# A transformer layer's output projection on Trainium2: loads issued earlier, scales made a tile ahead, stores on another queue, and the first up-projection slices without GpSimd

## The chip, the cores and the metric

The kernel runs on one core of a Trainium2 chip. A core has five engines with a fixed instruction order each: PE (TensorE, matrix products; its weight loads are shown apart as PEld), DVE (VectorE), ACT (ScalarE), POOL (GpSimd) and SP (SyncE, which here only issues transfers). They run beside each other and wait for one another through semaphores. Transfers between device memory and the core's own memory are issued by SP, ACT or POOL and carried by 16 DMA engines. The metric is the device time of one execution in microseconds (us); the time before is 3184.6, the median of 3 runs (3182.1 to 3186.07).

## The reference

One encoder layer over 2048 tokens of width 1024 (and 16 meta tokens ahead of them): two mixers side by side, latent attention with 8 heads and a bidirectional S5 state-space model, 512 channels each, then an output projection, and an MLP with squared ReLU. Cut to what the change touches:

```python
mix = jnp.concatenate([rms_norm(attn, g_mix[:512]), rms_norm(ssm, g_mix[512:])], axis=-1)
h = h + rms_norm(mix @ w_out, g_post_mix)
m = rms_norm(h, g_pre_mlp) @ w_mlp_up
m = jnp.square(jax.nn.relu(m)) @ w_mlp_down
h = h + rms_norm(m, g_post_mlp)
```

where `rms_norm(x, g)` is `x * rsqrt(mean(x²) + eps) * g`.

## The kernel before

**Stages.** Input projection; attention head by head with the S5 model woven in as a background task; the output projection with its norms; the MLP, whose up-projection starts with slices cut from the normed hidden state; the down-projection. All products are of float32 quality made from two halves: `split` (lines 124 to 126) rounds a tile to its high part on ACT (names with h: sh, ah, T00h) and subtracts that on DVE or POOL for the low part (sl, al, T00l); each product is then three matrix products (high·high, high·low, low·high).

**Memory scratch.** Attention writes its output, not yet divided, to AD and the sums of its weights to RD; after the last head of a block of 512 tokens the sums are read back, inverted on DVE (rr, line 648) and written to RD2. S5's gated output goes to SD. The residual after the output projection goes to HD, its normed and transposed form to HTD, from which the up-projection reads.

**The output projection** goes over 16 tiles of 128 tokens, t = 0 to 15. For each:

- `s_ops(t)` (line 1115) loads SD's columns into sr and makes sh, sl and sq, the per-token column sums of squares (square on ACT, sum on DVE, lines 1111 and 1112). sr has one buffer.
- `a_ops(t)` (line 1121) loads AD's columns into ar (two buffers) and the inverted sums, spread over partitions, into rb (one buffer, two transfers), multiplies them on DVE (line 1130), and makes ah, al and aq in the same way.
- `out_s(t)` makes S5's part of the projection, 24 products into two banks of 512 columns each (op, line 1184); `out_tile(t)` makes attention's part, 24 more into two other banks.
- The two RMS scales of a tile come from sq and aq: two tiny products with ones (ss, lines 1202 and 1203), a copy to s2c on DVE (line 1205), then on POOL a multiply-add and a power each (rs_v and rs_r, lines 131 and 132).
- For each 512 columns ACT multiplies attention's part by its scale (ot, line 1213) and DVE adds S5's part with its own (o, line 1214, two a tile). A square with its sum on ACT (jk, line 1218), a POOL scale, two DVE operations (lines 1220 and 1221, the gain gpo and the residual xt), the store to HD (line 1222), another square (line 1227), a POOL scale, and hn on DVE (line 1229).
- `hn_T(t)` transposes hn on PE (hT, line 1240) two tiles later, ACT copies it to hb (line 1245), and SP stores it to HTD (line 1246).

**Queues.** Every transfer of this stage is issued by SP, in one order: loads of sr, ar, rb and xt (lines 1118, 1124, 1128 and 1198) and the stores to HD and HTD. A transfer whose buffer or data isn't ready holds up those behind it in this order.

**The bridge to the MLP.** `t_slice(ct, k)` reads a slice traw of HTD (1 MB; line 1275) and makes seven split combinations of its four parts (T0k to T6k). Of its 11 subtractions 4 are on POOL (the splits of b11 and b22, and T1 and T4, lines 1312 and 1315), 7 on DVE. The weights' combinations st (line 1266) are on POOL too. The up-projection's products (p, line 1331) follow.

**What sets the order.** The order in which the code is written gives each instruction a place, and a scheduler with a timeline of its own moves instructions of an engine past each other ahead of the run; on the chip each engine's order is fixed. The results of products live in eight banks that are handed out in turn (`pa`), so a product can also wait for the reader of the bank's previous content.

Of the kernel before, what the change touches and what calls it, by code (L numbers as in the profile page):

```python
# [51 lines left out]
def hymba_layer_kernel(  # L52
# [71 lines left out]
    def split(src, h, l, eng=V):  # L124
        S.copy(out=h, in_=src)  # L125
        eng.tensor_tensor(out=l, in0=src, in1=f(h), op=ALU.subtract)  # L126
# [968 lines left out]
    def out_open():  # L1095
        ip = W["ip"] = ph.enter_context(pool("iO", 2, "right"))
        W["ep"] = ph.enter_context(pool("eO", 2, "right"))
        e1 = W["e1"] = ph.enter_context(pool("e1", 1, "right"))
        gpo = W["gpo"] = mk(e1, [128, D], "gpo")
        Y.dma_start(out=gpo, in_=g_post_mix[0].partition_broadcast(128))  # L1100
        for t in range(2):
            W["s", t] = s_ops(t)
            yield

    def halves(src, nm):

# [4 lines left out]
        S.activation(out=src, in_=src, func=AF.Square)  # L1111
        V.reduce_sum(out=sq, in_=src.rearrange("p k c -> p c k"), axis=AX.X)
        return h, l, sq

    def s_ops(t):
        cs = slice(t * 128, (t + 1) * 128)
        sr = W["ip"].tile([128, 4, 128], F32, tag="sr", name="sr", bufs=1)
        Y.dma_start(out=sr, in_=SD[:, cs].rearrange("(k p) c -> p k c", p=128))
        return halves(sr, "s")

    def a_ops(t):
        cs = slice(t * 128, (t + 1) * 128)
        ar = W["ip"].tile([128, 4, 128], F32, tag="ar", name="ar")
        Y.dma_start(out=ar, in_=AD[:, cs].rearrange("(k p) c -> p k c", p=128))
        rb = W["ip"].tile([128, 4, 128], F32, tag="rb", name="rb", bufs=1)
        for b in range(2):
            src = RD2[b:b + 1, cs]
            Y.dma_start(out=rb[64 * b:64 * b + 64],
                        in_=bass.AP(src.tensor, src.offset, [[0, 64], [2 * 2048, 4], [1, 128]]))
        V.tensor_tensor(out=ar, in0=ar, in1=rb, op=ALU.mult)  # L1130
# [48 lines left out]
    def out_mm(h, l, w0, half):
        hs = slice(half * 512, (half + 1) * 512)  # L1180
        p = pa("op")
        for k in range(4):
            for i, (a, b) in enumerate(((h, W["woh"]), (h, W["wol"]), (l, W["woh"]))):
                T.matmul(out=p, lhsT=a[:, k], rhs=b[:, w0 + k, hs], start=(k == 0 and i == 0),
                         stop=(k == 3 and i == 2))
        return p

    def out_s(t):
        h, l, sq = W.pop(("s", t))
        return sq, [out_mm(h, l, 4, half) for half in range(2)]  # L1190

    def out_tile(t, between):
        if t + 1 < NT:
            W["a", t + 1] = a_ops(t + 1)
        if t + 2 < NT:
            W["s", t + 2] = s_ops(t + 2)
        xt = W["e1"].tile([128, D], F32, tag="xt", name="xt")
        Y.dma_start(out=xt, in_=xv[t // 8, t % 8])
# [2 lines left out]
        p = pa("ss")
        T.matmul(out=p[:, 0:2], lhsT=sqa, rhs=ones)
        T.matmul(out=p[:, 2:4], lhsT=sqs, rhs=ones)
        s2 = sm.tile([128, 4], F32, tag="s2c", name="s2c")
        V.tensor_copy(s2, p[:, 0:4])
        ra = rstd_of(s2[:, 0:1], 512)
        rb = rstd_of(s2[:, 2:3], 512, eps=4 * EPS)
        o = W["ep"].tile([128, D], F32, tag="o", name="o")
        for half in range(2):
# [4 lines left out]
            V.scalar_tensor_tensor(out=o[:, hs], in0=ps[half], scalar=rb, in1=tm, op0=ALU.mult, op1=ALU.add)
# [5 lines left out]
        V.scalar_tensor_tensor(out=o, in0=o, scalar=r, in1=W["gpo"], op0=ALU.mult, op1=ALU.mult)  # L1220
        V.tensor_tensor(out=o, in0=o, in1=xt, op=ALU.add)
# [7 lines left out]
        V.scalar_tensor_tensor(out=hn, in0=o, scalar=r, in1=gpr, op0=ALU.mult, op1=ALU.mult)  # L1229
        return hn  # L1230

    def hn_T(t, hn):

        ct, i = t // 8, t % 8
        cs = slice((i % 4) * 128, (i % 4) * 128 + 128)
        ps = []
        for a in range(2):
# [4 lines left out]
            ps.append(p)
        b = hn if t == NT - 1 else mk(tq, [128, D], "hb")
        for a in range(2):
            S.copy(out=b[:, a * 512:(a + 1) * 512], in_=ps[a])
            Y.dma_start(out=HTD[ct].rearrange("k p b c -> p k b c")[:, :, 2 * a + i // 4, cs],
                        in_=b[:, a * 512:(a + 1) * 512].rearrange("p (k c) -> p k c", k=4))
# [29 lines left out]
    W["a", 0] = a_ops(0)
    for t in range(2):
        W["ps", t] = out_s(t)
    last = []  # L1280
    prep = up_prep(0)
    facs = []
# [20 lines left out]
        for n in range(7):  # L1303
            TB[n, k] = (mk(tb, [128, 512], f"T{n}{k}h", F32R), mk(tb, [128, 512], f"T{n}{k}l", F32R))

    def t_slice(ct, k):
# [4 lines left out]
        split(b11, *TB[B11, k], G)
        G.tensor_tensor(out=l[T1], in0=b12, in1=b11, op=ALU.subtract)
        V.tensor_tensor(out=l[T3], in0=b22, in1=b12, op=ALU.subtract)
        V.tensor_tensor(out=l[T2], in0=b22, in1=l[T1], op=ALU.subtract)
# [256 lines left out]
```

## Time and profile before

| what | value |
|---|---|
| median of 3 runs | 3184.6 us |
| the profiled execution's own time | 3184.3 us |
| its span in the profile | 3182.5 us |
| mean granted PE clock | 0.977 |
| PE, DVE, ACT, POOL busy, share of the span | 95%, 60%, 49%, 40% |
| from the first multiplication ar·rb (line 1130) to the first o of tile 15 (line 1214) | 1558.8 to 1821.3 us |
| PE busy in 1540 to 1900 us | 295.0 of 360 us |

The rows of the trace that are quoted below are of three kinds. A timeline row has the start and the length in us, the engine, the line of the kernel, the operation, the tile written and the tiles read, and in brackets how long the engine was idle before and what ended that. A row of the groups has the number of instructions, their busy time and the mean in ns. A row of a stretch has busy times by engine, the granted PE clock and the share of the DMA engines. SPq marks SP's issue of a transfer.

### The profile page before, as it was taken

What the parts mean: (1) busy time and instruction counts of PE and PEld (TensorE: products, weight loads), DVE (VectorE), ACT (ScalarE), POOL (GpSimd) and SP (SyncE); (2) the same over time, 40 slices, a digit from 0 to 9 for tenths busy, and PEclk for the clock granted to TensorE, in tenths of its full rate; (3) what the DMA queues carried; (4) which work ended last, traced back from release to release, by engine and by line L of the source; (5) the groups of instructions that cost most, each with busy time, mean ns of one, the idle gap of its engine ahead of it and who ended that gap; (6) DMA issues with size and microseconds to landing.
All of it is one profiled execution on the core that took longest, in us unless ns stands there. A gap on an engine that the chain in (4) does not pass through costs nothing. (4 is left out here: it accounts for less than half of the span.)

```text
span 3182.5 us, 42348 instructions
## 1 busy us (share of the span) xinstructions
PE 3017.4 (95%) x14455; PEld 2412.5 (76%) x14455; DVE 1914.8 (60%) x2989; ACT 1563.2 (49%) x2985; POOL 1268.3 (40%) x2363
## 2 busy tenths in 40 slices
PE   6999988899999999999879789998999999999998
PEld 5899965566777766788657568886888888888887
DVE  6333278888888889875356584449444234444447
ACT  4333346777777789864335455455544421111112
POOL 4221255776888887600032275457443000000002
PEclk8999989999999999999989889999999999999999
DMA  4232241111001123231356443333332422222216
GB/s 151 65 86 69 63 91 29 53 45 41 18 19 27 27 70 94 72 122 50 67 137 191 145 149 122 106 107 112 125 106 100 137 79 76 73 76 76 67 63 205
DMA packets 244377, 279.51 MB, mean 88 GB/s; under 512 B 35920, under 2 KB 180688, under 8 KB 243136
## 3 DMA queue, kind: packets, MB, share of 16 engines
q1 hardware_dynamic: 242112, 275.10, 28.5%
q8 instruction: 113, 1.85, 0.2%
q10 hardware_dynamic: 1792, 1.57, 0.2%
q14 instruction: 104, 0.85, 0.1%
q0 software_dynamic: 256, 0.14, 0.0%
HBM read 181.31 MB, written 95.36 MB: 87 GB/s over the span
## 5 line engine op out<-in xcount | busy, mean ns | idle before, releaser
L623 ACT ACTIVATE ph<-s 128x512 fp32r<-128x512 f32 (+1 forms) x544 | 324.1, 596 | 201.6 <-PE s L621 187.5
L627 DVE TENSOR_TENSOR pl<-s,ph 128x512 fp32r<-128x512 f32 x512 | 349.5, 684 | 110.5 <-ACT s L626 108.3
L1516 PE MATMUL dn<-dh,ah 128*128 128x512 f32 x1024 | 398.3, 389 | 0.0
L1516 PE MATMUL dn<-dl,ah 128*128 128x512 f32 x1024 | 398.3, 389 | 0.0
L1516 PE MATMUL dn<-dh,al 128*128 128x512 f32 x1024 | 398.2, 389 | 0.0
L574 DVE TENSOR_REDUCE mx<-mxp 128x1 f32<-128x512 f32 x512 | 342.9, 684 | 47.7 <-PE mxp L573 44.2
L626 ACT ACTIVATE s<-s 128x512 f32<-128x512 f32 x512 | 303.6, 593 | 0.7
L125 ACT CAST ah<-mraw 128x512 fp32r<-128x512 f32 x128 | 79.5, 621 | 449.9 <-DMA mraw<-MD 269.4
L1500 POOL TENSOR_TENSOR ss<-s2f 128x1 f32<-128x1 f32 x16 | 11.2, 699 | 702.2 <-ACT jk L1497 702.2
L1266 POOL TENSOR_TENSOR st<-raw 128x512 f32<-128x512 f32 x128 | 174.0, 1359 | 263.6 <-DVE al L126 263.5
L1521 DVE TENSOR_TENSOR acc<-dn,acc 128x512 f32<-128x512 f32 x224 | 153.3, 688 | 137.6 <-PE dn L1516 137.6
L611 PE MATMUL X<-pl,vt 128*65 128x512 f32 x512 | 207.3, 405 | 25.7 <-DVE pl L627 23.8
L619 PE MATMUL s<-ql,kh 96*128 96x512 f32 (+1 forms) x544 | 224.1, 412 | 4.1 <-ACT o L641 2.6
L1516 PEld LDWEIGHTS dn<-dh,ah 128*128 128x128 f32 x1024 | 192.2, 188 | 39.9
L1516 PEld LDWEIGHTS dn<-dh,al 128*128 128x128 f32 x1024 | 192.2, 188 | 39.9
L1516 PEld LDWEIGHTS dn<-dl,ah 128*128 128x128 f32 x1024 | 192.2, 188 | 39.9
L620 PE MATMUL s<-qh,kl 96*128 96x512 f32 (+1 forms) x544 | 217.2, 399 | 0.0
L621 PE MATMUL s<-qh,kh 97*128 97x512 f32 (+1 forms) x544 | 213.4, 399 | 0.0
L612 PE MATMUL X<-ph,vt 128*64 128x512 f32 x512 | 203.3, 397 | 0.0
L613 PE MATMUL X<-ph,vt 128*65 128x512 f32 x512 | 202.9, 396 | 0.0
L126 DVE TENSOR_TENSOR al<-mraw,ah 128x512 fp32r<-128x512 f32 x128 | 88.4, 691 | 189.8 <-ACT ah L125 179.7
L573 PE MATMUL mxp<-kh,qh 96*128 96x512 f32 x512 | 196.4, 405 | 5.4 <-DVE mx L574 1.9
(813 smaller groups left out, 7819.2 us busy)
## 6 DMA issues: line engine op xcount, KB each, us to landing
raw<-in_w_mlp_up_dram SPq DMA_DIRECT2D x32, 1024.0 KB
MD<-r SPq DMA_DIRECT2D x128, 256.0 KB
mraw<-MD SPq DMA_DIRECT2D x128, 256.0 KB
xt<-in_x_dram SPq DMA_DIRECT2D x32, 512.0 KB
raw<-in_w_mlp_down_dram SPq DMA_DIRECT2D x32, 512.0 KB
ug<-UD SPq DMA_DIRECT2D x32, 256.0 KB
HD<-o SPq DMA_DIRECT2D x16, 512.0 KB
traw<-HTD SPq DMA_DIRECT2D x8, 1024.0 KB
```

Of the source, the lines that this page charges most:

```text
L573: T.matmul(out=p, lhsT=qs[n][0][0:96, j * 128:(j + 1) * 128], rhs=kh[0:96, b * 512:(b + 1) * 512])
L574: V.reduce_max(out=mxs[n][:, j, b:b + 1], in_=p, axis=AX.X)
L611: T.matmul(out=X[:65], lhsT=v[:, t, 0:65], rhs=pl_, start=(t == 0), stop=False)
L612: T.matmul(out=X[:64], lhsT=v[:, t, 65:129], rhs=ph_, start=False, stop=False)
L613: T.matmul(out=X[:65], lhsT=v[:, t, 0:65], rhs=ph_, start=False, stop=False)
L619: T.matmul(out=s[:m], lhsT=kh[0:96, cs], rhs=ql, start=True, stop=False)
L620: T.matmul(out=s[:m], lhsT=kl[:, cs], rhs=qh[0:96], start=False, stop=False)
L621: T.matmul(out=s[:m], lhsT=kh[:, cs], rhs=qh, start=False, stop=True)
L623: S.activation(out=ph_[:m], in_=s[:m], func=AF.Exp, scale=SCALE)
L626: S.activation(out=s, in_=s, func=AF.Exp, scale=SCALE)
L627: V.tensor_tensor(out=pl_, in0=s, in1=f(ph_), op=ALU.subtract)
L1516: T.matmul(out=p, lhsT=a[:, ts_], rhs=c[:, hs], start=(q == 0 and w == 0), stop=(q == FB - 1 and w == 2))
```

## The change

What it does, part by part:

1. A new `loads(t)` issues the loads of sr, xt, ar and rb of a tile up to two tiles ahead of its use; xt, rb and sr now have two buffers instead of one (ar had two). `sd_load` makes the load of sr by itself.
2. A new `scales(t + 1)` makes the next tile's two RMS scales inside tile t, ahead of the transposes; s2c's copy moves from DVE to ACT.
3. `out_s(0)` is written ahead of attention's last products, `out_s(1)` behind them.
4. The store to HD moves from SP's queue to ACT's, behind the second square, and the stores to HTD move from SP's to ACT's.
5. The four slices of ct = 0 make all 11 subtractions on DVE; those of ct = 1 stay as they were.

```diff
+    def sd_load(t):
+        cs = slice(t * 128, (t + 1) * 128)
+        W["sr", t] = sr = W["ip"].tile([128, 4, 128], F32, tag="sr", name="sr")
+        Y.dma_start(out=sr, in_=SD[:, cs].rearrange("(k p) c -> p k c", p=128))
+
     def s_ops(t):
-        cs = slice(t * 128, (t + 1) * 128)
-        sr = W["ip"].tile([128, 4, 128], F32, tag="sr", name="sr", bufs=1)
-        Y.dma_start(out=sr, in_=SD[:, cs].rearrange("(k p) c -> p k c", p=128))
-        return halves(sr, "s")
-
-    def a_ops(t):
+        return halves(W.pop(("sr", t)), "s")
+
+    def loads(t):
+
+        if ("x", t) in W:
+            return
+        if ("sr", t) not in W and t > 1:
+            sd_load(t)
+        W["x", t] = xt = tq.tile([128, D], F32, tag="xt", name="xt", bufs=2)
+        Y.dma_start(out=xt, in_=xv[t // 8, t % 8])
         cs = slice(t * 128, (t + 1) * 128)
         ar = W["ip"].tile([128, 4, 128], F32, tag="ar", name="ar")
         Y.dma_start(out=ar, in_=AD[:, cs].rearrange("(k p) c -> p k c", p=128))
-        rb = W["ip"].tile([128, 4, 128], F32, tag="rb", name="rb", bufs=1)
+        rb = W["ip"].tile([128, 4, 128], F32, tag="rb", name="rb")
+        W["ar", t] = ar, rb
...
+    def a_ops(t):
+        ar, rb = W.pop(("ar", t))
         V.tensor_tensor(out=ar, in0=ar, in1=rb, op=ALU.mult)
         return halves(ar, "a")
...
+    for _ in bg:
+        pass
+    W["ps", 0] = out_s(0)
     for u in pend:
         u()
-    for _ in bg:
-        pass
+    W["ps", 1] = out_s(1)
...
+    def scales(t):
+
+        sqs = W["ps", t][0] if ("ps", t) in W else W["s", t][2]
+        p = pa("ss")
+        T.matmul(out=p[:, 0:2], lhsT=W["a", t][2], rhs=ones)
+        T.matmul(out=p[:, 2:4], lhsT=sqs, rhs=ones)
+        s2 = sm.tile([128, 4], F32, tag="s2c", name="s2c")
+        S.copy(out=s2, in_=p[:, 0:4])
+        W["r", t] = rstd_of(s2[:, 0:1], 512), rstd_of(s2[:, 2:3], 512, eps=4 * EPS)
 
     def out_tile(t, between):
+        for u in range(t + 1, t + 3):
+            if u < NT:
+                loads(u)
         if t + 1 < NT:
             W["a", t + 1] = a_ops(t + 1)
-        if t + 2 < NT:
-            W["s", t + 2] = s_ops(t + 2)
-        xt = W["e1"].tile([128, D], F32, tag="xt", name="xt")
-        Y.dma_start(out=xt, in_=xv[t // 8, t % 8])
+            if ("ps", t + 1) not in W:
+                W["s", t + 1] = s_ops(t + 1)
+        xt = W.pop(("x", t))
...
-        V.tensor_copy(s2, p[:, 0:4])
-        ra = rstd_of(s2[:, 0:1], 512)
-        rb = rstd_of(s2[:, 2:3], 512, eps=4 * EPS)
+        ra, rb = W.pop(("r", t))
...
+        if t + 1 < NT:
+            scales(t + 1)
         between()
...
-        Y.dma_start(out=HD[t], in_=o)
...
         S.activation(out=jk, in_=o, func=AF.Square, accum_out=ss)
+        S.dma_start(out=HD[t], in_=o)
...
-            Y.dma_start(out=HTD[ct].rearrange("k p b c -> p k b c")[:, :, 2 * a + i // 4, cs],
+            S.dma_start(out=HTD[ct].rearrange("k p b c -> p k b c")[:, :, 2 * a + i // 4, cs],
...
-    def t_slice(ct, k):
+    def t_slice(ct, k, eng):
...
-        split(b11, *TB[B11, k], G)
-        G.tensor_tensor(out=l[T1], in0=b12, in1=b11, op=ALU.subtract)
+        split(b11, *TB[B11, k], eng)
+        eng.tensor_tensor(out=l[T1], in0=b12, in1=b11, op=ALU.subtract)
...
-    t_slice(0, 0)
-    t_slice(0, 1)
-    up_pair_k(0, stepper(0), lambda k: t_slice(0, k + 2) if k < 2 else None)
+    t_slice(0, 0, V)
+    t_slice(0, 1, V)
+    up_pair_k(0, stepper(0), lambda k: t_slice(0, k + 2, V) if k < 2 else None)
```

The lines of the tile move: the multiplication ar·rb from 1130 to 1144, the products op from 1184 to 1165, ot and o from 1213 and 1214 to 1235 and 1236, s2c from 1205 to 1215, the HD store from 1222 to 1251, the HTD store from 1246 to 1270, the column sums from 1112 to 1113.

**How it moves instructions.** On DVE, where attention ends (pl and ph are attention's last weights, sl, al, sq and aq the output projection's first operands), the order before is:

```order
L1130 TENSOR_TENSOR ar<-ar,rb 128x512
L627 TENSOR_TENSOR pl<-s,ph 128x512
L126 TENSOR_TENSOR sl<-sr,sh 128x512
L126 TENSOR_TENSOR al<-ar,ah 128x512
L627 TENSOR_TENSOR pl<-s,ph 128x512
L1130 TENSOR_TENSOR ar<-ar,rb 128x512
L1112 TENSOR_REDUCE sq<-sr 128x128
L1112 TENSOR_REDUCE aq<-ar 128x128
L627 TENSOR_TENSOR pl<-s,ph 128x512
L632 TENSOR_TENSOR ph<-s,ph 16x512
L1130 TENSOR_TENSOR ar<-ar,rb 128x512
```

The three multiplications are those of tiles 1, 2 and 3. The same stretch of DVE with the change:

```order
L1144 TENSOR_TENSOR ar<-ar,rb 128x512
L627 TENSOR_TENSOR pl<-s,ph 128x512 x2
L1113 TENSOR_REDUCE aq<-ar 128x128
L126 TENSOR_TENSOR al<-ar,ah 128x512
L627 TENSOR_TENSOR pl<-s,ph 128x512
L1113 TENSOR_REDUCE aq<-ar 128x128
L1144 TENSOR_TENSOR ar<-ar,rb 128x512
L627 TENSOR_TENSOR pl<-s,ph 128x512
L1144 TENSOR_TENSOR ar<-ar,rb 128x512
L632 TENSOR_TENSOR ph<-s,ph 16x512
```

Two of attention's pl now stand between the multiplications of tiles 1 and 2 ahead of any column sum, and the multiplication of tile 3 stands ahead of attention's last ph, no longer behind it.

In the middle of the output projection one round of DVE before (from one tile's column sum to the next tile's two o):

```order
L1112 TENSOR_REDUCE aq<-ar 128x128
L1220 SCALAR_TENSOR_TENSOR o<-o,rs_r,gpo 128x1024
L1221 TENSOR_TENSOR o<-o,xt 128x1024
L1130 TENSOR_TENSOR ar<-ar,rb 128x512
L1205 COPY s2c<-ss 128x4
L126 TENSOR_TENSOR sl<-sr,sh 128x512
L1112 TENSOR_REDUCE sq<-sr 128x128
L1229 SCALAR_TENSOR_TENSOR hn<-o,rs_r,gpr 128x1024
L1214 SCALAR_TENSOR_TENSOR o<-op,rs_r,ot 128x512 x2
L126 TENSOR_TENSOR al<-ar,ah 128x512
```

and with the change, from about tile 6 on:

```order
L1113 TENSOR_REDUCE aq<-ar 128x128
L1236 SCALAR_TENSOR_TENSOR o<-op,rs_r,ot 128x512 x2
L1144 TENSOR_TENSOR ar<-ar,rb 128x512
L126 TENSOR_TENSOR sl<-sr,sh 128x512
L1113 TENSOR_REDUCE sq<-sr 128x128
L1244 SCALAR_TENSOR_TENSOR o<-o,rs_r,gpo 128x1024
L1245 TENSOR_TENSOR o<-o,xt 128x1024
L126 TENSOR_TENSOR al<-ar,ah 128x512
L1253 SCALAR_TENSOR_TENSOR hn<-o,rs_r,gpr 128x1024
```

The copy s2c is gone from DVE, the two o of a tile stand between the column sum and the multiplication, and all later steps of a tile (the gain, the residual, hn) stand behind the multiplication.

On SP one round of transfers before (x2 means two in a row):

```order
L1246 DMA HTD<-hb 128x4x128 x2
L1124 DMA ar<-AD 128x4x128
L1222 DMA HD<-o 128x1024
L1198 DMA xt<-in_x_dram 128x1024
L1128 DMA rb<-RD_78 64x4x128 x2
L1118 DMA sr<-SD 128x4x128
```

and on ACT a round with the change, where the stores now stand:

```order
L1250 ACTIVATE jk,ss<-o 128x1024
L1251 DMA HD<-o 128x1024
L1215 COPY s2c<-ss 128x4
L1269 COPY hb<-hT 128x512
L1112 ACTIVATE ar<-ar 128x512
L1269 COPY hb<-hT 128x512
L1235 ACTIVATE ot<-op,rs_r 128x512
L1270 DMA HTD<-hb 128x4x128 x2
L1235 ACTIVATE ot<-op,rs_r 128x512
```

The HD store stands between the second square and the copy of the scales, the two HTD stores between the two ot of a tile; SP's round keeps ar, xt, rb and sr alone.

More of the change, by code (lines that the diff above doesn't have):

```diff
@@ L1113, in halves @@
         return h, l, sq
+    def sd_load(t):
+        cs = slice(t * 128, (t + 1) * 128)
+        W["sr", t] = sr = W["ip"].tile([128, 4, 128], F32, tag="sr", name="sr")
+        Y.dma_start(out=sr, in_=SD[:, cs].rearrange("(k p) c -> p k c", p=128))
     def s_ops(t):
[L1116 to L1121 removed]
+        return halves(W.pop(("sr", t)), "s")
[3 more added lines that the diff above has]
+        if ("sr", t) not in W and t > 1:
+            sd_load(t)
+        W["x", t] = xt = tq.tile([128, D], F32, tag="xt", name="xt", bufs=2)
+        Y.dma_start(out=xt, in_=xv[t // 8, t % 8])
         cs = slice(t * 128, (t + 1) * 128)
@@ L1144, in bg_step, with out_mm, out_s @@
         return next(bg, None)
+    def out_mm(h, l, w0, half):
+        hs = slice(half * 512, (half + 1) * 512)
+        p = pa("op")
+        for k in range(4):
+            for i, (a, b) in enumerate(((h, W["woh"]), (h, W["wol"]), (l, W["woh"]))):
+                T.matmul(out=p, lhsT=a[:, k], rhs=b[:, w0 + k, hs], start=(k == 0 and i == 0),
+                         stop=(k == 3 and i == 2))
+        return p
+    def out_s(t):
+        h, l, sq = W.pop(("s", t))
+        return sq, [out_mm(h, l, 4, half) for half in range(2)]
     for n in range(len(seq)):
@@ L1177, in hymba_layer_kernel @@
     Y.dma_start(out=gpr, in_=g_pre_mlp[0].partition_broadcast(128))
[L1179 to L1190, printed above, removed]
+    def scales(t):
[6 more added lines that the diff above has]
+        W["r", t] = rstd_of(s2[:, 0:1], 512), rstd_of(s2[:, 2:3], 512, eps=4 * EPS)
     def out_tile(t, between):
+        for u in range(t + 1, t + 3):
+            if u < NT:
+                loads(u)
         if t + 1 < NT:
             W["a", t + 1] = a_ops(t + 1)
-        if t + 2 < NT:
-            W["s", t + 2] = s_ops(t + 2)
-        xt = W["e1"].tile([128, D], F32, tag="xt", name="xt")
-        Y.dma_start(out=xt, in_=xv[t // 8, t % 8])
+            if ("ps", t + 1) not in W:
+                W["s", t + 1] = s_ops(t + 1)
+        xt = W.pop(("x", t))
         sqs, ps = W.pop(("ps", t), None) or out_s(t)
         h, l, sqa = W.pop(("a", t))
[L1201 to L1205, printed above, removed]
-        ra = rstd_of(s2[:, 0:1], 512)
-        rb = rstd_of(s2[:, 2:3], 512, eps=4 * EPS)
+        ra, rb = W.pop(("r", t))
         o = W["ep"].tile([128, D], F32, tag="o", name="o")
@@ L1275, in s_load @@
         Y.dma_start(out=raw, in_=HTD[ct, k])
+    loads(0)
     W["a", 0] = a_ops(0)
-    for t in range(2):
-        W["ps", t] = out_s(t)
+    scales(0)
     last = []
@@ L1310, in t_slice @@
         l = {n: rt() for n in (T1, T3, T2, T4)}
-        split(b11, *TB[B11, k], G)
-        G.tensor_tensor(out=l[T1], in0=b12, in1=b11, op=ALU.subtract)
+        split(b11, *TB[B11, k], eng)
+        eng.tensor_tensor(out=l[T1], in0=b12, in1=b11, op=ALU.subtract)
         V.tensor_tensor(out=l[T3], in0=b22, in1=b12, op=ALU.subtract)
         V.tensor_tensor(out=l[T2], in0=b22, in1=l[T1], op=ALU.subtract)
-        G.tensor_tensor(out=l[T4], in0=l[T2], in1=b21, op=ALU.subtract)
+        eng.tensor_tensor(out=l[T4], in0=l[T2], in1=b21, op=ALU.subtract)
         split(l[T2], *TB[T2, k])
@@ L1320, in t_slice @@
         split(l[T4], *TB[T4, k])
-        split(b22, *TB[B22, k], G)
+        split(b22, *TB[B22, k], eng)
         if (ct, k + 2) in ((ct, 2), (ct, 3)):
@@ L1438, in hymba_layer_kernel @@
     s_load(1, 1)
-    up_pair_k(NP - 1, stepper(NP - 1), lambda k: t_slice(1, k))
+    up_pair_k(NP - 1, stepper(NP - 1), lambda k: t_slice(1, k, G))
     up_pair_k(NP, stepper(NP), lambda k: None)
```

## The prediction

> **What bounds the kernel now.** I read the page's busy table first, then the table of stretches from 1540 to 1900 us (the columns: stretch, length, busy time of PE, its weight loads, DVE, ACT and POOL, granted clock, DMA share, GB/s).
>
> ```profile
> PE 3017.4 (95%) x14455; PEld 2412.5 (76%) x14455; DVE 1914.8 (60%) x2989; ACT 1563.2 (49%) x2985; POOL 1268.3 (40%) x2363
> ```
> ```profile
> 1560.00:1580.00 20.00, 14.12 (x46) 9.76 (x46) 9.27 (x14) 7.96 (x16) 0.00 (x0) 0.83 0.27 64
> ...
> 1700.00:1720.00 20.00, 19.23 (x91) 14.95 (x90) 13.44 (x17) 11.25 (x20) 4.87 (x12) 1.00 0.67 161
> ...
> 1820.00:1840.00 20.00, 6.51 (x17) 4.27 (x17) 14.42 (x12) 10.53 (x19) 10.87 (x11) 0.50 0.40 123
> 1840.00:1860.00 20.00, 14.06 (x48) 9.23 (x48) 19.92 (x16) 6.65 (x13) 16.87 (x11) 0.90 0.30 106
> ...
> 1880.00:1900.00 20.00, 19.68 (x88) 15.94 (x87) 14.73 (x19) 12.08 (x22) 13.06 (x9) 1.00 0.61 204
> ```
>
> PE is the bound nearly everywhere, at 95% of the span. This change touches the stretch in which it is not: it starves where attention ends (1560), runs almost full in the middle of the output projection (1700), starves at its end (1820) and while the first up-projection slices are made (1840), and is full again from 1880 on. Only time won or lost up to there counts.
>
> **Start of the stage.** The DVE's timeline there, then the queue of SP, an ACT row and a PE row (start, length, engine, line, operation; in brackets the idle time before it and who ended it).
>
> ```profile
> 1558.82 0.69 DVE L1130 TENSOR_TENSOR ar<-ar,rb 128x512 f32<-128x512 f32 x1 [7.63 <-DMA rb<-RD]
> ...
> 1568.62 0.69 DVE L1130 TENSOR_TENSOR ar<-ar,rb 128x512 f32<-128x512 f32 x1 [4.59 <-DMA rb<-RD]
> ...
> 1577.95 0.69 DVE L1130 TENSOR_TENSOR ar<-ar,rb 128x512 f32<-128x512 f32 x1 [5.83 <-DMA rb<-RD]
> ...
> 1581.12 0.68 DVE L632 TENSOR_TENSOR ph<-s,ph 16x512 fp32r<-16x512 f32 x1
> 1588.33 0.69 DVE L1130 TENSOR_TENSOR ar<-ar,rb 128x512 f32<-128x512 f32 x1 [6.52 <-DMA ar<-AD]
> ...
> 1602.73 0.35 DVE L648 RECIPROCAL rr<-rr 128x32 f32<-128x32 f32 x1 [11.14 <-DMA rr<-RD]
> ...
> 1604.69 0.75 DVE L1214 SCALAR_TENSOR_TENSOR o<-op,rs_r,ot 128x512 f32<-128x512 f32 x1 [1.06 <-POOL rs_r L132]
> ```
> ```profile
> 1548.48 1.33 SPq L1128 DMA_DIRECT2D rb<-RD  x2
> ...
> 1559.54 1.25 SPq L1128 DMA_DIRECT2D rb<-RD  x2
> ```
> ```profile
> 1590.31 0.58 ACT L641 COPY o<-X 65x512 f32<-65x512 f32 x1
> ```
> ```profile
> 1581.15 0.69 PE L611 MATMUL X<-pl,vt 128*65 128x512 f32 x1 [4.59 <-DVE pl L627]
> ```
>
> The four multiplications ar·rb stand in the DVE's fixed order among attention's last weights (pl, ph), so what they wait for, PE waits for. They come some 10 us apart because rb has one buffer: the second load goes out at 1559.54, just after the first multiplication has freed it, and lands 9.1 us later. The copy of the last head, 1590.31, then starts a trip through memory (store, load, reciprocal, 1602.73) that POOL waits for too, and the first o of tile 0, which I call o0(0), comes at 1604.69: 14.4 us after the copy.
>
> With two rb buffers the second load no longer waits for a multiplication; its landing lies between 1560 (beside the first) and 1568 (as now); I take 1564. The third rb load goes out when multiplication 0 frees a buffer, 1559.5, and by the 9.1 us above lands near 1569. Then ar(2) and ar(3) decide: their buffers come free with the column sums aq(0) and aq(1), near 1567 and 1569.5, and loads of 4 to 6.5 us (the latter from the 6.52 row) put multiplications 2 and 3 at about 1573 and 1575.5. The changed order has ph behind multiplication 3, not 2, so ph stands near 1576.5; sl(2), a square and the copy follow by 1578.5. The trip is the same, 14.4 us: o0(0) at about 1592.7. **Term 1: −12 us**; bounds 0 (nothing gained) to −17, if nothing is left of the three later waits (4.59, 5.83 and 6.52). Moving `out_s(0)` ahead of attention's last products I put at nothing: the order has 32 of S5's products among those already before the change and 38 after it, six more, 6 × 0.21 = 1.3 us on a PE that waits there for the DVE (the 4.59 of its row), and 1.3 it costs or gives if that cover goes.
>
> **Rounds of the stage.** One round in steady state, and the later o0 rows.
>
> ```profile
> 1692.96 1.07 DVE L1112 TENSOR_REDUCE aq<-ar 128x128 f32<-128x512 f32 x1 [1.70 <-ACT ar L1111]
> 1693.95 1.27 DVE L1220 SCALAR_TENSOR_TENSOR o<-o,rs_r,gpo 128x1024 f32<-128x1024 f32 x1
> 1695.27 1.23 DVE L1221 TENSOR_TENSOR o<-o,xt 128x1024 f32<-128x1024 f32 x1
> 1697.52 0.69 DVE L1130 TENSOR_TENSOR ar<-ar,rb 128x512 f32<-128x512 f32 x1 [1.03 <-DMA ar<-AD]
> 1698.13 0.15 DVE L1205 COPY s2c<-ss 128x4 f32<-128x4 f32 x1
> 1698.20 0.68 DVE L126 TENSOR_TENSOR sl<-sr,sh 128x512 fp32r<-128x512 f32 x1
> 1699.58 1.08 DVE L1112 TENSOR_REDUCE sq<-sr 128x128 f32<-128x512 f32 x1 [0.70 <-ACT sr L1111]
> 1700.57 1.28 DVE L1229 SCALAR_TENSOR_TENSOR hn<-o,rs_r,gpr 128x1024 f32<-128x1024 f32 x1
> 1701.76 0.75 DVE L1214 SCALAR_TENSOR_TENSOR o<-op,rs_r,ot 128x512 f32<-128x512 f32 x1
> ...
> 1715.01 0.75 DVE L1214 SCALAR_TENSOR_TENSOR o<-op,rs_r,ot 128x512 f32<-128x512 f32 x1
> ```
> ```profile
> 1644.84 0.75 DVE L1214 SCALAR_TENSOR_TENSOR o<-op,rs_r,ot 128x512 f32<-128x512 f32 x1 [0.44 <-POOL rs_r L132]
> ...
> 1740.39 0.75 DVE L1214 SCALAR_TENSOR_TENSOR o<-op,rs_r,ot 128x512 f32<-128x512 f32 x1 [0.44 <-POOL rs_r L132]
> 1744.98 0.69 DVE L1130 TENSOR_TENSOR ar<-ar,rb 128x512 f32<-128x512 f32 x1 [3.83 <-DMA ar<-AD]
> ...
> 1760.84 0.74 DVE L1214 SCALAR_TENSOR_TENSOR o<-op,rs_r,ot 128x512 f32<-128x512 f32 x1
> ...
> 1821.27 0.75 DVE L1214 SCALAR_TENSOR_TENSOR o<-op,rs_r,ot 128x512 f32<-128x512 f32 x1 [0.44 <-POOL rs_r L132]
> ```
> ```profile
> 1690.90 0.93 SPq L1246 DMA_DIRECT2D HTD<-hb  x2
> 1694.07 0.36 SPq L1124 DMA_DIRECT2D ar<-AD  x1
> ...
> 1736.66 0.39 SPq L1124 DMA_DIRECT2D ar<-AD  x1
> ```
>
> A round takes 13.25 us (1701.76 to 1715.01). It is a loop through a load: the column sum aq frees ar's buffer, SP issues the next ar (1694.07), and the multiplication behind it on the DVE lands L = 3.45 us later (1697.52); all that stands behind it waits. Before the change that loop is 9.8 + L. PE alone needs 12.3: in the stretch from 1700 to 1720 its 91 instructions took 19.23 us, 0.211 each, and a tile has 48 products, 8 transposes and 2 scale sums. It has little slack to give.
>
> First rounds: o0(0) to o0(2) now takes 40.15 us, two and a half steady rounds too long by 13.6; s2c's copy stands there on the DVE behind a waiting multiplication, and PE's next bank waits for it. In the changed order that copy is on ACT and no bank waits for the DVE in this way. I take two rounds of 16 for it, between 13.3 and the 20.45 us of the row pair 1740.39 and 1760.84. **Term 2: −8 us** (bounds 0 and −13.5).
>
> Rounds 2 to 15: now 176.4 us (1644.84 to 1821.27). In the changed order the load of ar is asked for two tiles ahead, but ar has two buffers as before: tile t+4's load still waits for the sum of tile t+2. Up to about tile 6, four or five DVE operations (3.9 to 5 us) stand between that sum and the multiplication, which cover a load of 4; from tile 6 to 12 only the two o operations do, and the load shows. There the loop is: multiplication 0.6, sl 0.6, wait 0.7 and sq 1.0, the two products on o 2.5, the second square with its scale about 3.4 (an estimate: hn follows the add's end by 4.1 now, with a multiplication, s2c, sl and sq between; in the changed order an HD issue, the scale copy and two small POOL operations are put into that path instead), hn 1.2, aq 1.0: 11 + L. I take L = 4, the 3.45 of the row and half a microsecond because the two HTD stores now go out just before ar, not 2.2 us earlier. So four rounds at 13.25, six at 15, three last ones without loads at PE's 12.3: 53 + 90 + 37, and 3 us for the two 1 MB traw loads, which now cost 20.45 − 13.3 = 7.1. Sum 183. **Term 3: +6.6 us**, with L between 2.4 (rounds of 13.3) and 8.3 (1736.66 to 1744.98, the row behind the traw loads): −7 to +32.
>
> Past the last tile nothing changes: PE's first up-projection product waits for a cast on ACT behind tile 15's squares, 8.8 us after o0(15).
>
> ```profile
> 1830.03 0.79 PE L1331 MATMUL p<-T00h,ah 128*128 128x512 f32 x1 [7.12 <-ACT T00h L125]
> ```
>
> The HD and HTD stores move from SP's queue to ACT's. On ACT they cost three issues of about 0.46 us a tile (two take 0.93), beside 8 to 11 busy of 20; SP loses the waits for hb that stood ahead of ar. I count that only through L. The Trainium skill speaks against more: its page "DMA: Bandwidth & Descriptors", section "Issuing engines are not separate DMA queues", says that transfers started by different engines run on the same 16 DMA engines and interleave, so that a second issuer saves just the issue time. By that rule ar still shares with the stores and the sum goes to rival 1; no row of this run has a store on ACT's queue in this stage to show it.
>
> **First up-projection slices.** DVE rows beside POOL's work and without it, and the last one of the slices.
>
> ```profile
> 1837.25 1.76 DVE L126 TENSOR_TENSOR T21l<-traw,T21h 128x512 fp32r<-128x512 f32 x1
> ...
> 1847.37 0.68 DVE L126 TENSOR_TENSOR T50l<-r,T50h 128x512 fp32r<-128x512 f32 x1
> 1847.97 0.68 DVE L1314 TENSOR_TENSOR r<-traw,r 128x512 f32<-128x512 f32 x1
> ...
> 1873.21 1.18 DVE L126 TENSOR_TENSOR T53l<-r,T53h 128x512 fp32r<-128x512 f32 x1
> ```
>
> The slices run from 1831.6 to 1874.4, 42.8 us, with the DVE full; an operation takes 1.76 us beside a POOL one and 0.68 (0.60 from start to start) without. The change gives the DVE 44 slice operations instead of 28, and 6 splits of weights stand among them: 50 × 0.60 = 30.2, plus six subtractions of the weights that stay on POOL, each slowing one by 1.08: 36.7. Two traw loads still wait for a slice to end; I add 3. **Term 4: −3 us** (−7 to +2).
>
> **Sum.** −12 − 8 + 6.6 − 3 = −16.4, from the profiled execution's 3184.3 (span 3182.5 and 1.8 around it), which lies 0.3 under the median of the runs: **3168**.
>
> **Rivals.** 1. *The gain is given back at the stores.* The load lands 5.7 us after the HTD stores' issue (1691.83 to 1697.52); if it is the stores that pace it, L is 5.6 once they go out right ahead: six rounds at 16.6, term 3 +16, time 3177. For it: the DMA share of 0.67 in mid-stage; against: two queues can take turns. 2. *Slower:* L reaches the 8.3 us of the traw row in every round, since the loads, now early and in a bunch, fall together with HD, HTD and xt: six rounds at 19.3, term 3 about +33, time 3194. It decides from L = 4 + 16.4/6 = 6.7 on; against it, only two rounds have such a value now, each behind 2 MB. 3. *Loads land sooner* without stores ahead of them in their queue: ten rounds of 13.25 and the last 37, 169.5: term 3 −7, time 3154. 4. *The change doesn't do what it says:* rb was not what held the start, the loads just take turns: multiplication 3 at 1585, term 1 −3, time 3177. For it: the 6.52 there is a wait for ar; against: the three before are for rb.
>
> **How the numbers follow.** Forecast (3160 to 3176) 0.52; rival 1 0.20; rival 2 0.09; rival 3 0.12; rival 4 0.07. The range reaches from 3150 (rival 3 with the slices at their −7) to 3183 (rival 1 with half of term 1); rival 2 and the outer half of the others lie outside. A measurement tells about 0.2%, 6.4 us, from no change: faster is the forecast, rival 3 and half of rivals 1 and 4, 0.77; same the other halves, 0.14; slower 0.09.
>
> **What would show it.** Term 1: multiplications 0 to 3 end by about 1576 and the copy L641 comes near 1578 rather than 1590. Term 2: no product of op waits for s2c; o0(2) near 1625. Term 3: gaps between o0 rows of 13.3, then 15, and idle time ahead of the multiplication from tile 10 on. Term 4: slices' DVE rows mostly at 0.68, T53l by about 40 us after T00. Wrong it is if the gaps in mid-stage are at 12.3 (loads hidden) or above 16.7.

## The result, and the profile after

| what | before | after |
|---|---|---|
| median of 4 runs | 3185.3 us (3182.1 to 3186.7) | 3161.6 us (3159.2 to 3165.2) |
| the profiled execution's own time, its span | 3184.3, 3182.5 | 3162.8, 3160.6 |
| mean granted PE clock | 0.977 | 0.976 |

The ratio is 0.9929, with a 95% interval of 0.9914 to 0.9944: 23.8 us faster, where 3168 had been forecast with 3150 to 3183 around it. In another set of runs beside others (e11 below) the ratio was 0.9930 (0.9918 to 0.9943).

One thing has to be taken out before the two traces are laid side by side. The last store of S5's output ahead of the loads stands at 1542.02 in the trace of before and here in that of after, both from SP's timeline:

```profile
1542.02 0.32 SPq L1090 DMA_DIRECT2D SD<-sv  x1
```
```profile
1544.48 0.32 SPq L1090 DMA_DIRECT2D SD<-sv  x1
```

The stage begins 2.5 us later in the execution after, by what came before it; in the other runs it begins from 3 us earlier to 5 us later than before the change. So lengths within the stage are compared, and where a moment is given for both, the 2.5 us are named.

**The start.** DVE's timeline after, where attention ends, and the copy of the last head on ACT:

```profile
1560.17 0.69 DVE L1144 TENSOR_TENSOR ar<-ar,rb 128x512 f32<-128x512 f32 x1 [5.44 <-DMA rb<-RD]
...
1564.53 0.69 DVE L1144 TENSOR_TENSOR ar<-ar,rb 128x512 f32<-128x512 f32 x1
...
1576.98 0.69 DVE L1144 TENSOR_TENSOR ar<-ar,rb 128x512 f32<-128x512 f32 x1 [7.21 <-DMA ar<-AD]
...
1578.19 0.68 DVE L1144 TENSOR_TENSOR ar<-ar,rb 128x512 f32<-128x512 f32 x1
1578.91 0.68 DVE L632 TENSOR_TENSOR ph<-s,ph 16x512 fp32r<-16x512 f32 x1
...
1591.51 0.35 DVE L648 RECIPROCAL rr<-rr 128x32 f32<-128x32 f32 x1 [3.75 <-DMA rr<-RD]
1591.89 0.75 DVE L1236 SCALAR_TENSOR_TENSOR o<-op,rs_r,ot 128x512 f32<-128x512 f32 x1
```
```profile
1583.39 0.58 ACT L641 COPY o<-X 65x512 f32<-65x512 f32 x1 [2.41 <-PE X L608]
```

The four multiplications are done in 18 us instead of 29.5; one long wait is left, 7.21 us for the load of ar, ahead of the third. The copy comes at 1583.39 instead of 1590.31, the first o at 1591.89 instead of 1604.69.

**The rounds.** The first o of tiles 2, 6, 12 and 15, from the same timeline:

```profile
1624.11 0.75 DVE L1236 SCALAR_TENSOR_TENSOR o<-op,rs_r,ot 128x512 f32<-128x512 f32 x1
...
1677.91 0.75 DVE L1236 SCALAR_TENSOR_TENSOR o<-op,rs_r,ot 128x512 f32<-128x512 f32 x1 [1.46 <-ACT ot L1235]
...
1778.18 0.74 DVE L1236 SCALAR_TENSOR_TENSOR o<-op,rs_r,ot 128x512 f32<-128x512 f32 x1
...
1808.80 0.75 DVE L1236 SCALAR_TENSOR_TENSOR o<-op,rs_r,ot 128x512 f32<-128x512 f32 x1 [2.04 <-ACT ot L1235]
```

On average these are four rounds of 13.5 us, six of 16.7 and three of 10.2: 184.7 us from tile 2 to tile 15, where before it was 176.4. So the middle of the stage became slower. The average of the first four hides two kinds: they took 17.1, 9.2, 11.5 and 16.0 us, and in the first and the last of them DVE stood idle ahead of the multiplication for over 6 us, which came 7.3 and 10.5 us behind the issue of its ar. (The profile names no releaser for these two waits.) DVE's rows, then SP's:

```profile
1638.79 0.69 DVE L1144 TENSOR_TENSOR ar<-ar,rb 128x512 f32<-128x512 f32 x1 [6.19 <-issue]
...
1671.72 0.69 DVE L1144 TENSOR_TENSOR ar<-ar,rb 128x512 f32<-128x512 f32 x1 [6.63 <-issue]
```
```profile
1631.49 0.36 SPq L1134 DMA_DIRECT2D ar<-AD  x1
...
1661.20 0.36 SPq L1134 DMA_DIRECT2D ar<-AD  x1
```

How the six slow rounds go, one of them shows: DVE's rows, then the transfers that SP and ACT issue in it.

```profile
1695.53 1.05 DVE L1113 TENSOR_REDUCE aq<-ar 128x128 f32<-128x512 f32 x1
1696.49 0.74 DVE L1236 SCALAR_TENSOR_TENSOR o<-op,rs_r,ot 128x512 f32<-128x512 f32 x1
1697.99 0.75 DVE L1236 SCALAR_TENSOR_TENSOR o<-op,rs_r,ot 128x512 f32<-128x512 f32 x1 [0.76 <-ACT ot L1235]
1703.66 0.69 DVE L1144 TENSOR_TENSOR ar<-ar,rb 128x512 f32<-128x512 f32 x1 [4.92 <-DMA ar<-AD]
```
```profile
1691.76 0.35 SPq L1131 DMA_DIRECT2D xt<-in_x_dram  x1
1696.61 0.36 SPq L1134 DMA_DIRECT2D ar<-AD  x1
```
```profile
1691.87 0.34 ACTq L1251 DMA_DIRECT2D HD<-o  x1
...
1693.54 0.37 ACTq L1270 DMA_DIRECT2D HTD<-hb  x1
...
1694.54 1.41 ACTq L1270 DMA_DIRECT2D HTD<-hb  x1
```

The load of ar, issued at 1696.61, lets the multiplication go at 1703.66: L, the time from the issue of ar to its multiplication, is 7.05 us where it was 3.45. In the six rounds it is 6.8, 7.05, 6.3, 5.8, 8.1 (behind the two traw loads) and 3.8. Ahead of the load at 1696.61, within 5 us, went xt and HD (512 KB each) and the two HTD stores (256 KB each). The table of the DMA engines shows the same as a burst. Its first line is their busy share in tenths in 40 slices, its second what they moved; first before (1690 to 1717 us), then after (1690 to 1720):

```profile
DMA  6897999995299995677323599965703999953344
GB/s 34 29 83 65 159 262 300 282 309 164 101 394 316 225 358 221 77 49 43 31 44 84 130 266 338 276 192 163 225 21 146 400 249 243 413 187 49 42 47 43
```
```profile
DMA  1142100144899999861002444589689999999840
GB/s 45 29 44 34 36 23 21 60 131 162 281 404 388 388 356 287 243 179 42 0 0 42 44 45 44 34 35 23 12 44 161 333 416 442 367 335 345 271 126 21
```

Before, less than 60 GB/s move for no more than 3 us on end. After, no more than 60 GB/s move for 6 to 9 us on end, then up to 440, and ar is the last in line.

**The end.** PE's first up-projection product comes at 1818.19 instead of 1830.03, with the same wait for a cast; the slices' last split at 1855.34 instead of 1873.21:

```profile
1818.19 0.80 PE L1355 MATMUL p<-T00h,ah 128*128 128x512 f32 x1 [5.42 <-ACT T00h L125]
```
```profile
1855.34 0.68 DVE L126 TENSOR_TENSOR T53l<-r,T53h 128x512 fp32r<-128x512 f32 x1
```

The slices run from 1820.9 to 1856.0, 35.1 us instead of 42.8. From clock to clock the start and the first two rounds made 20.7 us, the rounds from tile 2 to 15 took 8.3 back, the way from the first o of tile 15 to the slices took another 1.7 (12.1 us instead of 10.4), and the slices made 7.7: 18.4 of the 21.9 us that lie between the two spans. The rest lies behind the slices and was not followed.

### The profile page after: what moved, and what is told of

It reads as the page before. It is cut to its first block, busy times and chain, and to the rows that moved or that the text cites. A ratio compares the mean times of both kernels' runs of the same rounds, so it can differ in the third digit from the quotient of the medians.

```text
span 3160.6 us, 42309 instructions
## 1 busy us (share of the span) xinstructions
PE 3011.7 (95%) x14455; PEld 2415.0 (76%) x14455; DVE 1906.4 (60%) x2989; ACT 1566.2 (50%) x3001; POOL 1244.3 (39%) x2347
## 5 line engine op out<-in xcount | busy, mean ns | idle before, releaser
L1290 POOL TENSOR_TENSOR st<-raw 128x512 f32<-128x512 f32 x128 | 182.6, 1427 | 274.1 <-DVE al L126 271.3
L1524 POOL TENSOR_TENSOR ss<-s2f 128x1 f32<-128x1 f32 x16 | 11.2, 699 | 702.2 <-ACT jk L1521 702.2
```

## The experiments

Each is an edit of the changed kernel; times are medians, the ratio is to the kernel before on the same chip, where the changed kernel has 0.9929 and 0.9930. Within 0.002 or so of that two kernels can't be told apart by their times.

**e4_rb1: one buffer for rb.**

```diff
-        rb = W["ip"].tile([128, 4, 128], F32, tag="rb", name="rb")
+        rb = W["ip"].tile([128, 4, 128], F32, tag="rb", name="rb", bufs=1)
```

> The changed kernel with one buffer for rb instead of two. Theory 1 (the second buffer of rb is what shortens the start): multiplications 1 to 3 come again 8 to 10 us apart, the copy of the last head goes back from 1583 to about 1589 to 1593, time 3168 to 3172; later rounds as now, as rb lands well ahead there. Theory 2 (the start is shorter because of the other parts: sr's second buffer, the loads' order): the copy stays within 2 us, time 3160 to 3164.

3183.9 us, ratio 0.9984 (0.9974 to 0.9993): some 17 us of the gain are gone. From the last store of S5's output to the first o it is 54.3 us instead of 41.5 (56.8 before the change). The multiplications in its DVE timeline:

```profile
1557.35 0.69 DVE L1144 TENSOR_TENSOR ar<-ar,rb 128x512 f32<-128x512 f32 x1 [5.99 <-DMA rb<-RD]
...
1567.08 0.69 DVE L1144 TENSOR_TENSOR ar<-ar,rb 128x512 f32<-128x512 f32 x1 [5.32 <-DMA rb<-RD]
...
1577.55 0.69 DVE L1144 TENSOR_TENSOR ar<-ar,rb 128x512 f32<-128x512 f32 x1 [5.23 <-DMA ar<-AD]
...
1586.50 0.69 DVE L1144 TENSOR_TENSOR ar<-ar,rb 128x512 f32<-128x512 f32 x1 [6.94 <-DMA rb<-RD]
```

They are again 9 to 10.5 us apart, and the copy came at 1588.5. Theory 1 holds, but its price was set too low: the rounds of that kernel are longer as well (193.1 us from tile 2 to 15, 8.4 more), which no theory here had.

**e2_stores_sp: HD and HTD back on SP's queue.**

```diff
-        S.dma_start(out=HD[t], in_=o)
+        Y.dma_start(out=HD[t], in_=o)
-            S.dma_start(out=HTD[ct]...
+            Y.dma_start(out=HTD[ct]...
```

> The changed kernel with both stores, HD and HTD, back on SP's queue. Theory 1 (it is the bytes in flight that make the load of ar slow, whatever queue they come from): the load still takes 5.5 to 7 us from issue to the multiplication, the time stays within 4 us of 3161.5. Theory 2 (two queues in turn slow the load, where one queue would have let it come right behind the stores): the load takes 3.5 to 4 as before the change, six rounds of 14, about 3146. Theory 3 (SP's waits for hb and o hold the loads up, which is what the move was to end): the load goes out later, rounds of 17 to 19, 3165 to 3175.

3171.5 us, ratio 0.9946 (0.9933 to 0.9958). A round of its SP queue, and the multiplication that follows:

```profile
1694.49 0.35 SPq L1131 DMA_DIRECT2D xt<-in_x_dram  x1
1694.89 0.42 SPq L1251 DMA_DIRECT2D HD<-o  x1
1696.27 2.46 SPq L1270 DMA_DIRECT2D HTD<-hb  x2
1699.34 0.82 SPq L1134 DMA_DIRECT2D ar<-AD  x1
```
```profile
1706.88 0.69 DVE L1144 TENSOR_TENSOR ar<-ar,rb 128x512 f32<-128x512 f32 x1 [5.40 <-DMA ar<-AD]
```

L is 7.5, with one queue as with two: theory 2 falls, as it is not the second queue that makes the load late; the burst, which both kernels have, is left. SP issues ar right after the sum here too. The time is about 5 us longer, which is within what can't be told apart; in the trace the rounds from tile 2 to 6 take longer (60.7 us instead of 53.8), which theory 3 would have, but why was not followed. The Trainium skill's page "DMA: Bandwidth & Descriptors", section "Issuing engines are not separate DMA queues", has it that a second issuer saves only issue time; the load of ar agrees, with 7.05 and 7.5 us in these two runs. Whether the 5 us are that saving isn't shown.

**e3_htd_sp: only HTD back on SP.** The second half of the edit above.

> The changed kernel with the HTD stores alone back on SP's queue, HD left on ACT's. Theory 1 (bytes in flight, whatever the queue): within 4 us of 3161.5, load of ar 5.5 to 7 us. Theory 2 (two queues in turn): the load comes down to 4 to 5, rounds of 15, about 3152. Theory 3 (SP held up by hb): 3165 to 3172.

3164.8 us, ratio 0.9927 (0.9914 to 0.9939): no difference, waits ahead of the multiplication of 2.9 to 6.0 us in the six rounds. Theory 1.

**e5_ar3_xt1: a third buffer for ar, one for xt.** A third buffer for ar alone (e1_ar3) gave no result: it leaves 14.5 KB per partition where the tiles that follow need 16. So xt gives one up here.

```diff
-        W["x", t] = xt = tq.tile([128, D], F32, tag="xt", name="xt", bufs=2)
+        W["x", t] = xt = tq.tile([128, D], F32, tag="xt", name="xt", bufs=1)
-        ar = W["ip"].tile([128, 4, 128], F32, tag="ar", name="ar")
+        ar = W["ip"].tile([128, 4, 128], F32, tag="ar", name="ar", bufs=3)
```

> The changed kernel with a third buffer for ar and, to make room, one for xt. The DVE's order stays. In the changed kernel xt, HD, two HTD and ar, 2 MB together, go out within 5 us, ar last, and its 256 KB take 6 to 7 us. Theory 1 (ar stands last in this burst, since its buffer comes free with the column sum): with a free buffer it goes out 4 us earlier, second in the burst, lands before the two o are done, waits ahead of the multiplication from o0(6) to o0(12) below 2 us, rounds of 12.5 to 13.5 instead of 16.7; less what the last three tiles lose (10 to 12 each): 3140 to 3150. Theory 2 (the DMA engines are the bound of the round, whoever comes first): rounds stay at 16 or more, time 3156 to 3164.

3168.0 us, ratio 0.9953 (0.9941 to 0.9966): slower than without. It didn't test what it was made for. The scheduler used the third buffer to put every multiplication a tile earlier in DVE's order, so that the load again waits for the sum just ahead of it, and still goes out 5 us behind xt:

```profile
1685.75 0.35 SPq L1131 DMA_DIRECT2D xt<-in_x_dram  x1
1690.73 0.36 SPq L1134 DMA_DIRECT2D ar<-AD  x1
```

At the start a fifth multiplication, which waited 7.1 us for its load, came to stand ahead of the first o, and that one came at 1597.0.

**e9_am: the product in a tile of its own.** What e5 meant, by another way: the multiplication writes to a new tile am with one buffer, so that ar and rb come free with it; the loads of ar and rb are written first, xt (one buffer) last.

```diff
-        if ("sr", t) not in W and t > 1:
-            sd_load(t)
-        W["x", t] = xt = tq.tile([128, D], F32, tag="xt", name="xt", bufs=2)
-        Y.dma_start(out=xt, in_=xv[t // 8, t % 8])
...
+        if ("sr", t) not in W and t > 1:
+            sd_load(t)
+        W["x", t] = xt = tq.tile([128, D], F32, tag="xt", name="xt", bufs=1)
+        Y.dma_start(out=xt, in_=xv[t // 8, t % 8])
...
-        V.tensor_tensor(out=ar, in0=ar, in1=rb, op=ALU.mult)
-        return halves(ar, "a")
+        am = W["ip"].tile([128, 4, 128], F32, tag="am", name="am", bufs=1)
+        V.tensor_tensor(out=am, in0=ar, in1=rb, op=ALU.mult)
+        return halves(am, "a")
```

> The changed kernel with the product ar*rb written to a tile of its own (one buffer), so that ar and rb come free with the multiplication and not with the column sum; in SP's order ar and rb go out right behind the multiplication, a round ahead of their use, and xt (one buffer, to make room) last. Theory 1 (in the changed kernel the load of ar stands last in a burst of 2 MB behind xt, HD and HTD, and the six rounds with loads are paced by it): the waits ahead of the multiplication fall below 1 us, rounds 2 to 15 take 12.3 to 13.3 each, as PE or DVE paces them, o0(2) to o0(15) some 165 instead of 185, the start is 0 to 6 us shorter too: 3135 to 3148. Theory 2 (the bytes of a round pace it, the DMA engines being shared): rounds of 15 and more, 3155 to 3165.

3135.2 us, ratio 0.9838 (0.9824 to 0.9851): 30 us faster than the changed kernel beside it. A round of its DVE, a load in its SP queue, and a stretch of its table (length, then PE's busy time):

```profile
1689.01 0.74 DVE L1237 SCALAR_TENSOR_TENSOR o<-op,rs_r,ot 128x512 f32<-128x512 f32 x1
1689.67 0.68 DVE L1145 TENSOR_TENSOR am<-ar,rb 128x512 f32<-128x512 f32 x1
...
1701.33 0.74 DVE L1237 SCALAR_TENSOR_TENSOR o<-op,rs_r,ot 128x512 f32<-128x512 f32 x1
1701.99 0.68 DVE L1145 TENSOR_TENSOR am<-ar,rb 128x512 f32<-128x512 f32 x1
```
```profile
1690.38 0.36 SPq L1130 DMA_DIRECT2D ar<-AD  x1
```
```profile
1660.00:1680.00 20.00, 20.00 (x96) 16.78 (x95) 14.15 (x16) 10.03 (x19) 3.96 (x11) 1.00 0.86 217
```

No multiplication waits from tile 3 on, the rounds from tile 7 to tile 13 are 12.3 us but for one, and PE is full in the stretch shown. Tile 2 to 15 takes 160.1 us instead of 184.7. The same bytes move in a round, but ar goes out right behind a multiplication, nearly two rounds ahead of its own (that at 1714.30). That settles theory 1: the load of ar paced the rounds of the changed kernel. One buffer for xt is not what helped, as e5 has it too; the new order of the loads and the new tile were not tested apart. The start gains too (the copy at 1575.4: the load of ar for multiplication 2 no longer waits for a column sum, and multiplication 3 stands behind attention's last weights). One round of 21.4 us is left, in which the two traw loads (2 MB) go out ahead of xt:

```profile
1729.07 1.23 DVE L1246 TENSOR_TENSOR o<-o,xt 128x1024 f32<-128x1024 f32 x1 [5.39 <-DMA xt<-in_x_dram]
```

**e10_am_dve: e9 with s2c's copy on DVE. e13_am_traw: e10 with the traw loads written behind the last tile.**

> The kernel of the run before with the copy of the scale sums on DVE besides. Theory 1 (once the load no longer paces the rounds, POOL's 2.0 us ahead of hn count, part of which is ACT's copy behind the HD store's issue): hn comes 0.5 to 1 us sooner in a round, 5 to 10 us off rounds 2 to 15 unless PE paces them. Theory 2 (PE paces them): within 3 us of the run before.

> The kernel of run e10 with the loads of the first two slices written behind the last tile, which the scheduler turns into one load a round instead of two at once. Theory 1 (in e9 and e10 the round of 20 to 21 us is the two traw loads, 2 MB ahead of xt in SP's queue): the round of 20 splits into two of 14 to 15, 2 to 5 us off, 3128 to 3131 against 3132.5. Theory 2 (SP's other loads or ACT's stores wait for the slices' loads all the same): within 2 us.

3132.5 (0.9821, interval 0.9807 to 0.9834) and 3132.3 (0.9827, 0.9811 to 0.9843): neither differs from e9 by what can be told; in both, most rounds of the middle are at 12.3 us, as in e9. In e13 the round with traw still takes 20.5 us: the two loads stood apart in SP's order by only ar and rb, so the edit did not spread them over two rounds, and its theories stay untested. How to get that round down stays open.

**e6_slices_pool: the first slices' four subtractions back on POOL.** `t_slice(0, k, V)` becomes `t_slice(0, k, G)` for all four.

> The changed kernel with the first slices' four subtractions back on POOL. Theory 1 (the DVE is slowed to 1.76 us beside POOL and frees nothing): the slices take some 43 us instead of 35, time 3167 to 3171. Theory 2 (the slices are paced by ACT's casts, the traw loads and PE's products): at most 3 us, up to 3165.

3172.0 us, ratio 0.9960 (0.9946 to 0.9973), about 9 us of the gain. Most rows of its first slices are at 1.76 us again, and the last split comes 41 us after the first row of the slices; theory 1.

```profile
1826.53 1.77 DVE L126 TENSOR_TENSOR T21l<-traw,T21h 128x512 fp32r<-128x512 f32 x1
...
1861.79 0.68 DVE L126 TENSOR_TENSOR T53l<-r,T53h 128x512 fp32r<-128x512 f32 x1
```

**e7_s2c_dve: s2c's copy on DVE. e12_scales_in_tile: the scales made in their own tile again. e8_outs_late: `out_s(0)` behind attention's last products.**

```diff
-        S.copy(out=s2, in_=p[:, 0:4])
+        V.tensor_copy(s2, p[:, 0:4])
```
```diff
         xt = W.pop(("x", t))
+        scales(t)
         sqs, ps = W.pop(("ps", t), None) or out_s(t)
...
-        if t + 1 < NT:
-            scales(t + 1)
         between()
...
-    scales(0)
```
```diff
-    W["ps", 0] = out_s(0)
     for u in pend:
         u()
+    W["ps", 0] = out_s(0)
```

> The changed kernel with the copy of the scale sums on DVE instead of ACT, the scales still a tile ahead. Theory 1 (the copy on DVE holds a bank and PE behind a waiting multiplication, as before the change): PE waits for s2c in several rounds, early rounds 3 to 5 us longer, time 3165 to 3170. Theory 2 (a tile ahead, the copy's place does not matter; on ACT it sits behind the second square just as well): within 3 us of 3161.5, or faster by 2 to 4, as hn's scale no longer waits on POOL behind ACT's copy.

> The changed kernel with a tile's two scales made in the tile itself again, behind which its first o waits; the copy stays on ACT. Theory 1 (a tile ahead, the scales are off the path from PE's products to o): the first rounds are some 4 us longer in all and the last three, where no load paces, 11 to 12 each instead of 9 to 12, 3167 to 3175. Theory 2 (the load of ar paces the rounds anyway, and the scheduler had room to put the scales early): within 3 us of 3163.5.

> The changed kernel with S5's first products written behind attention's last ones, as before the change. Theory 1 (the order had most of them ahead already, 32 against 38): within 3 us of 3161.5. Theory 2 (what is written earlier also moves the loads and operands of the first tiles): the copy of the last head comes 3 us or more later, time 3165 or more.

3158.3 (0.9921, 0.9908 to 0.9935), 3159.9 (0.9915, 0.9899 to 0.9930) and 3163.2 (0.9936, 0.9924 to 0.9949): none can be told from the changed kernel. In e12 the six rounds with loads came down to 12.6 to 17.4 us and the last three went up to 11.2 to 12.5, with no effect on the time that can be told: the scales a tile ahead speed up the tail, and the middle is slower with them. In e7 PE does wait for s2c (seven waits, 20.9 us), as it does for ACT's copy in the changed kernel (six, 20.2): the copy's place does not change that.

**e11_changed_again:** the changed kernel beside e9 and e10.

> The changed kernel once more, beside the two runs before it on the same chip: every theory expects 3157 to 3165, a ratio to before of 0.993.

3166.0 us, ratio 0.9930 (0.9918 to 0.9943).

## Why the prediction was right, and where it was not

The time came out 6 us below the forecast 3168, and term by term it was −15.3, −8, +8.3 and −7.7 us where −12, −8, +6.6 and −3 stood. Three causes were named rightly: rb's one buffer at the start, the load of ar behind the column sum in the middle, POOL beside DVE in the slices. That the sum came so near is luck in part, as the terms show.

**Term 1 (start, −12).** Measured −12.8 from clock to clock, −15.3 with the 2.5 us taken out; e4 shows rb's second buffer as the cause of most of it (12.8 us come back with one buffer). Inside the term two errors met. With the 2.5 us taken out, the multiplications came nearly where they were put (1557.7, 1562.1, 1574.5 and 1575.7; forecast were 1558.8, 1564, 1573 and 1575.5), the last two because the loads of ar went out earlier and took longer: multiplication 2 came 9.1 us behind their issue at 1567.92, and I had taken 4 to 6.5; two sr, two rb and two ar went out within 8 us there (SP's rows from 1562 to 1570). The copy was 5 us later than forecast by the clock, 2.4 with the 2.5 taken out. The trip from the copy to o0(0), which I had left at 14.4, took 8.5. Before, three loads, among them 1 MB of weights, were issued within 1.5 us of the head's last store; after, SP issued its next load 2.7 us after it. That these loads were in the way is argued, not tested; over the other runs the trip took from 6.6 to 13.0.

**Term 2 (first two rounds, −8).** 32.2 us, as forecast (two rounds of 16), but by luck, as the reason, s2c's copy off DVE, is not it: e7 and e12 keep two early rounds of 34.5 and 35.5, where the changed kernel itself had 33.5 in e11, and PE still waits for s2c, which was to be gone. What shortened them was not separated.

**Term 3 (rounds 2 to 15, 183).** 184.7, and in its parts: 53.8 for four rounds (53), 100.3 for six with the traw loads (93), 30.6 for three (37). Right is that ar's load, with two buffers, still waits for the column sum and paces the middle: e9 takes that wait away, and 24.6 us with it. What was not right, and what made up for it:

- The four early rounds agree by luck. The operations that were to cover the load there did not: two of these rounds had waits of 6.2 and 6.6 us and took 17.1 and 16.0, the two between took 9.2 and 11.5.
- L was 6.3 us on average over the six rounds, not 4; the rest of the loop, put at 11, took 9.0 to 10.4. I had added half a microsecond for the HTD stores and had not seen that DVE's new order (gain, residual, hn, sum in one run) sends xt and HD, 1 MB more, out ahead of ar in each round, where before they went out behind it (at 1696.90 and 1696.52, behind ar's 1694.07).
- Rival 2 had named this bunch, at 8.3 us, which only the round behind the traw loads came near (8.1). Rival 1 had the price nearly right (5.6) but put it to the stores alone; e2 and e3 show that their queue does not matter. That the bytes ahead of ar make L long is argued from the table of the DMA engines; no run took xt or HD alone out of the burst.
- By the forecast's own sum the longer L alone would have cost 14 us and left 3 of the gain of 16.4. What kept the gain are the six rounds (6.5 us shorter than that sum has them), the last three (6.4), and terms 1 and 4. The last three I had at PE's 12.3, and they took 12.3, 9.0 and 9.3. They are as short in e9, where PE is full in the middle, and took 12.5, 11.2 and 11.2 in e12: it is the scales made a tile ahead, for which I had no term, that shorten the last two.

**Term 4 (slices, −3).** −7.7. The count and the 0.60 us were right, and five operations were slowed by one on POOL, not six; without the 3 us for the traw loads, which did not come, the forecast would have been 36.7 for the 35.1 measured. e6 confirms the cause, 0.0030 of the ratio, 9 us. That nothing changes past the last tile was not quite so: the 1.7 us to the slices are not in the sum.

**The other edits.** `out_s(0)`, put at nothing, was nothing (e8). The scales a tile ahead, which had no term, change the tail and the middle but not the time by what can be told (e12), and s2c's place, on which term 2 rested, does not change it either (e7). The stores on ACT's queue were put at nothing but for L; whether they are worth the 5 us of e2 can't be told.

**Slips in the working.** The 40.15 us are compared with two steady rounds, not two and a half. 50 × 0.60 is 30.0, not 30.2. An L of 2.4 gives six rounds of 13.4 and a term of −3; the −7 is rival 3's, with ten rounds of 13.25. None of them changes the forecast by more than 0.2 us.

## What to carry to other kernels

A load asked for earlier in the code goes out no earlier than its buffer comes free: look for what frees the buffer, and for what else that moment sends out. Writing a product to its own tile, so that its inputs come free with it, and loading those first, was worth more here (30 us) than the whole change. Where steps are put closer together, look at the transfers they issue: here they bunched too, and the load at the end of the burst was the one that DVE waited for. And an average over rounds can agree with a forecast where no single round does.

## What the runs showed of the hardware that was not expected

A load of 256 KB (ar) took 3.45 us from issue to use with the transfers ahead of it spread over a round, and 7.05 us as the last of 1.75 MB issued within 5 us, at 287 to 404 GB/s in the five slices of that burst in which the DMA engines were busiest. An issue held up an engine: in e9 ACT's next ot waited 6.0 us, which the profile puts down to a traw load, but it began right at the end of an issue of two HTD stores that took 4.76 us on ACT.

```profile
1713.38 4.76 ACTq L1271 DMA_DIRECT2D HTD<-hb  x2
1718.19 0.69 ACT L1236 ACTIVATE ot<-op,rs_r 128x512 f32<-128x512 f32 x1 [5.96 <-DMA traw<-HTD]
```
